# Output projection of a hybrid decoder layer: which engine subtracts and scales, and in which order the second half's products run

## The chip, the cores and the metric

One core of one Trainium2 chip. The time is device microseconds of one execution. Engines: TensorE (PE, its weight loads PEld), VectorE (DVE), ScalarE (ACT), GpSimd (POOL), and SyncE (SP), which here issues DMAs only.

## The reference, cut to what matters

One layer over 1088 tokens (1024 of a prompt, 64 decode tokens), model width 1024, all in float32:

```python
h = x + jnp.concatenate([o_r, o_s], axis=-1) @ w_out
hf = rms_norm(h, norm_ffn_gain)
h = h + jnp.square(jax.nn.relu(hf @ w_up)) @ w_down
```

`o_r` is the retention mixer (8 heads, per-head norm, gate), `o_s` sliding-window attention; each is 512 wide, and `w_out` is 1024 x 1024. `w_up` is 1024 x 4096, `w_down` 4096 x 1024. The outputs also hold the retention states and the window caches.

## The kernel before, in words

Products are made exact enough by splitting: an operand becomes a high part (a rounding cast on ScalarE, line 786) and a low part (source minus high part, a subtraction on VectorE, line 787; `halve`). A product is three matmuls: high x high, low x high and high x low (`mm3`, lines 172 to 174).

Feature-major layout: a tile holds 128 features by tokens. Tokens fall into two halves s = 0, 1 of 544, each of two quarters of Q = 272. The stages are: input projection, attention, retention with the output projection of s = 0 worked into its last three blocks (`out_early`), the output projection of s = 1, then 16 up steps (`up`) and five groups of down products. Up and down use a seven-product scheme: the 2 x 2 block matrix (features in two halves by tokens in two quarters) enters as seven combinations of blocks, so the normalised-to-be rows are needed as operands B11, B21, B22 and the differences T1 to T4.

The output projection of a half makes eight tiles m = 0..7 of 128 output features. For each m, and for each quarter h, 24 matmuls accumulate in one PSUM bank: 12 from the attention half of the input (`a`, weights `woa`) and 12 from the retention half (`r`, weights `wor`). The weights come in pairs (m, m+1) over SP into a ring of three raw tiles (`wo_pair`, line 818) and are split into a ring of four (`wsplit`). `psM` gives eight banks in turn.

- `residual(s, m, pss)`, lines 830 to 853: POOL loads x into one of two `y` buffers (832), DVE adds the two banks (834), which also empties them, POOL stores y to `y_d` for the end of the kernel (836), and f = y * g_ffn is written (842). The returned `squares` squares y on ACT (847, 850) and adds it on DVE to `acc[s]` (851).
- `operands(s, m)`, lines 866 to 887: for a pair m, m + 4 (kk = m % 4) the splits into the operands (`put`, seven) and four differences on POOL (876, 881, 883, 885). The splits read f, some of the differences overwrite f in place.
- `norm(s)`, lines 889 to 897: sums of `acc[s]` over the features by column sums on PE (line 152 through `col_sums`, called at 894), then a power on POOL (132).
- `norm_spread`, lines 899 to 909: PE spreads the result over the partitions (905), ACT copies it to `rsf`. It is used only in `up` (1105).

The driver is lines 1044 to 1076. It first makes the `a` halves of m = 0..3 for s = 1 (all eight banks), then the operands of s = 0 for m = 2, 6, 3, 7. The loop over pairs then makes the `r` halves of (0, 1) and (2, 3), and `a` with `r` for (4, 5) and (6, 7), each followed by `residual`, the remaining operands of s = 0 (list `rest`) and `operands(1, m)`. `norm(0)` follows the pair (2, 3), `norm_spread(0)` the pair (4, 5). With the last pair, the first up weights are loaded, two sums of them made on POOL (1060, 1061) and four of them split; further sums are made at line 1032.

The order of instructions on each engine is made when the program is built: a scheduler simulates the program and takes on each engine, among the instructions that it holds ready, the one written first (`schedule_with_timeline_sim`); `issue_after` ties an instruction behind another. On the chip each engine then keeps to that order.

Of the kernel before, what the change touches and what calls it, by code (L numbers as in the profile page):

```python
# [13 lines left out]
AF = mybir.ActivationFunctionType  # L14
ALU = mybir.AluOpType
# [21 lines left out]
def hymba_layer(ctx: ExitStack, tc: tile.TileContext, a: dict, o: dict):  # L37
    nc = tc.nc
# [19 lines left out]
    def cload(name):  # L58
        t_ = const.tile(list(a[name].shape), F32, name="c_" + name)
        nc.sync.dma_start(t_, a[name])  # L60
        return t_
# [42 lines left out]
    g_ffn = cload("g_ffn")  # L104
# [26 lines left out]
    def rsqrt_inplace(ap, n):  # L131
        nc.gpsimd.tensor_tensor(ap, ap, mhalf.broadcast_to([P, n]), ALU.pow)
# [16 lines left out]
    def col_sums(out, src, rhs):  # L149

        for q in range(0, 128, 32):
            nc.tensor.matmul(out[q : q + 32], src[:, q : q + 32], rhs, start=True, stop=True)
# [34 lines left out]
    def bank(name):  # L187
        pool, tag, n = banks[turn[0] % 8]
        turn[0] += 1
        return pool.tile([P, 512], F32, tag=tag, bufs=n, name=name)  # L190
# [316 lines left out]
    for blk in range(4):  # L507
        w = wload(a["w_in"][3 + blk], 8, f"wqk{blk}")
        dst = qr_d if blk < 2 else kr_d
        for j in range(2):  # L510
            m = (blk % 2) * 2 + j
# [273 lines left out]
    def halve(hi, lo, src, lo_eng):  # L785
        nc.scalar.copy(hi, src)  # L786
        lo_eng.tensor_tensor(lo, src, hi.bitcast(F32), ALU.subtract)  # L787
# [6 lines left out]
    def rawload(src, name, tag="raw", pl=None):  # L794
        if tag == "rawb":
            t_ = ope.tile([P, 4, Q], F32, tag="op" + ("6h", "2h", "2l", "5h", "5l", "6l", "1h", "1l")[kept[0] % 8], name=name)
            raw = t_.rearrange("p k n -> p (k n)")[:, :1024]
            kept[0] += 1
        else:
            raw = mw.tile([P, 1024], F32, tag=tag, name=name, bufs=3)  # L800
        nc.scalar.dma_start(raw, src)
        return raw
# [11 lines left out]
    def wo_pair(s, m, half):  # L814

        raw = mw.tile([P, 1024], F32, tag="raw", name=f"wo{half}{s}_{m}_raw", bufs=3)
        c0 = 512 * (half == "a")
        nc.sync.dma_start(
            raw.rearrange("p (m n) -> p m n", m=2), a["w_out"][m : m + 2, :, c0 : c0 + 512].rearrange("m p n -> p m n")
        )  # L820
        for i in range(2):
            yield wsplit(raw[:, i * 512 : i * 512 + 512], "wa", f"wo{half}{s}_{m + i}", nc.vector)

    def out_half(s, half, ps, h, w, first, last):
        for k in range(4):
            lh, ll = (w[:, i, k * 128 : k * 128 + 128] for i in range(2))
            mh, ml = (mix[s, half + x][:, k, h, :] for x in "hl")
            last_out[0] = mm3(ps, lh, ll, mh, ml, first and k == 0, last and k == 3)

    def residual(s, m, pss):  # L830
        y = om.tile([P, 2, Q], F32, tag="y", name=f"y{s}_{m}", bufs=2)
        nc.gpsimd.dma_start(y.rearrange("p h n -> p (h n)"), a["xY"][:, s, m, :])
        for h in range(2):
            nc.vector.tensor_tensor(y[:, h, :], pss[h], y[:, h, :], ALU.add)
        kk, k2 = m % 4, m // 4
        nc.gpsimd.dma_start(y_d[:, 2 * k2 : 2 * k2 + 2, kk, s, :], y)
        if m > 5 and s == 0:
            f = mx0.tile([P, 2, Q], F32, tag=f"f{m}", name=f"f{s}_{m}")
        else:
            f = om.tile([P, 2, Q], F32, tag=f"f{min(m, 4)}", name=f"f{s}_{m}", bufs=1 + m // 4)  # L840
        fs[s, m] = f
        nc.vector.tensor_scalar(f, y, g_ffn[:, m : m + 1], None, ALU.mult)

        def squares():
            if m == 0:
                acc[s] = mw.tile([P, 2, Q], F32, tag="acc", name=f"acc{s}")
                nc.scalar.activation(acc[s], y, AF.Square)
            else:
                sq = om.tile([P, 2, Q], F32, tag="sq", name=f"sq{s}_{m}")
                nc.scalar.activation(sq, y, AF.Square)  # L850
                nc.vector.tensor_tensor(acc[s], acc[s], sq, ALU.add)

        return squares

    def out_parts(s, ms, half, psum, pss):

        for m in ms:
            if m % 2 == 0:
                gen = wo_pair(s, m, half)
            w = next(gen)  # L860
            for h in range(2):
                if half == "a":
                    pss[m, h] = psum()
                out_half(s, half, pss[m, h], h, w, half == "a", half == "r")

    def operands(s, m):

        kk, k2 = m % 4, m // 4
        f = fs[s, m]

        def put(i, src):
            halve(ops[i][s][0][:, kk, :], ops[i][s][1][:, kk, :], src, nc.vector)

        if k2 == 0:
            put(B11, f[:, 0, :])
            nc.gpsimd.tensor_tensor(f[:, 0, :], f[:, 1, :], f[:, 0, :], ALU.subtract)
            put(T1, f[:, 0, :])
        else:
            put(B21, f[:, 0, :])
            b12, t1 = fs[s, kk][:, 1, :], fs[s, kk][:, 0, :]  # L880
            nc.gpsimd.tensor_tensor(t1, f[:, 1, :], t1, ALU.subtract)
            put(T2, t1)
            nc.gpsimd.tensor_tensor(b12, f[:, 1, :], b12, ALU.subtract)
            put(T3, b12)
            nc.gpsimd.tensor_tensor(f[:, 0, :], f[:, 0, :], t1, ALU.subtract)
            put(T4, f[:, 0, :])
            put(B22, f[:, 1, :])

    def norm(s):

        ps = psM.tile([P, 512], F32, tag="b", name=f"psr{s}")
        for h in range(2):
            for i, r in enumerate((0, 128, 144)):
                col_sums(ps[:, 3 * h + i : 3 * h + i + 1], acc[s][:, h, r : r + 128], ones[:, 0:1])
        rf = (rst, nsinks)[s][:, 0:6]
        nc.vector.tensor_scalar(rf, ps[:, :6], 1.0 / 1024.0, EPS, ALU.mult, ALU.add)
        rsqrt_inplace(rf, 6)
# [124 lines left out]
    def left(order, src, name, lo_eng, raw_tag="raw", raw_pool=None, s_tag="S", s_pool=None, tags=("wa", "wb"), raws=None, sums=None):  # L1022

        r1, r2 = raws or (
            rawload(src[:, i * 1024 : i * 1024 + 1024], f"{name}_r{i + 1}", raw_tag, raw_pool) for i in range(2)
        )
        a11, a12, a21, a22 = r1[:, :512], r1[:, 512:], r2[:, :512], r2[:, 512:]
        have = {1: a11, 2: a12, 4: a22, **(sums or {})}

        def comb(i, p_, q_, op):  # L1030
            t_ = have[i] = (s_pool or mid).tile([P, 512], F32, tag=s_tag, name=f"{name}_s{i}", bufs=10 if s_tag == "Sb" else 4)
            nc.gpsimd.tensor_tensor(t_, p_, q_, op)

        for n, i in enumerate(order):
            if i in (5, 6) and 5 not in have:
                comb(5, a21, a22, ALU.add)
                comb(6, have[5], a11, ALU.subtract)
            if i == 7:
                comb(7, a11, a21, ALU.subtract)
            if i == 3:  # L1040
                comb(3, a12, have[6], ALU.subtract)
            yield wsplit(have[i], tags[n % len(tags)], f"{name}_w{i}", lo_eng)

    late = lambda: bank("pso")
    operand_tiles(0)
    pss = {}
    out_parts(1, range(4), "a", late, pss)
    for m in (2, 6, 3, 7):
        operands(0, m)
    mx0x.close()  # L1050
    operand_tiles(1)
    rest = [0, 4, 1, 5]
    for ms in ((0, 1), (2, 3), (4, 5), (6, 7)):
        if ms[0] > 3:
            out_parts(1, ms, "a", late, pss)
        out_parts(1, ms, "r", late, pss)
        if ms == (6, 7):
            r0 = [rawload(a["w_up"][0][:, i * 1024 : i * 1024 + 1024], f"wu0_r{i + 1}") for i in range(2)]
            s56 = mw.tile([P, 1024], F32, tag="raw", name="wu0_s56", bufs=3)
            nc.gpsimd.tensor_tensor(s56[:, :512], r0[1][:, :512], r0[1][:, 512:], ALU.add)  # L1060
            nc.gpsimd.tensor_tensor(s56[:, 512:], s56[:, :512], r0[0][:, :512], ALU.subtract)
            gen0 = left(
                PROD, None, "wu0", nc.vector, tags=("wa", "wa", "wa", "wa", "wb", "wb", "wb"), raws=r0,
                sums={5: s56[:, :512], 6: s56[:, 512:]})
            ready = [next(gen0) for _ in range(4)]
        for m in ms:
            squares = residual(1, m, [pss[m, h] for h in range(2)])
            if rest:
                operands(0, rest.pop(0))
            operands(1, m)  # L1070
            squares()
        if ms == (2, 3):
            norm(0)
        if ms == (4, 5):
            norm_spread(0, last_out[0])
    ox.close()

# [293 lines left out]
```

## Time and profile before

| | |
|---|---|
| median of 3 runs | 1210.6 us (1209.35 to 1212.11) |
| profiled execution | 1210.2 us, span 1208.4 us |
| granted PE clock, mean over the span | 0.996 |
| matmuls of the output projection, s = 0 | 383.7 to 448.3 us |
| the same, s = 1 | 448.3 to 504.9 us |
| first matmul of the up steps | 504.9 us |

Times on the trace are microseconds from the span's start. In a timeline row stand the start, the time taken, the engine, the line, the operation, its output and inputs, the shape and the count; in brackets the idle time of the engine ahead of it and what ended that. A row of instruction groups ends with the busy time in all, the mean nanoseconds of one, and the idle time ahead of them with its releasers. A row of windows gives for each engine the busy time in that window and, in brackets, the number of instructions, then the granted clock, the share of the DMA engines and GB/s.

### The profile page before, as it was taken

What the parts mean: (1) busy time and instruction counts of PE and PEld (TensorE: products, weight loads), DVE (VectorE), ACT (ScalarE), POOL (GpSimd) and SP (SyncE); (2) the same over time, 40 slices, a digit from 0 to 9 for tenths busy, and PEclk for the clock granted to TensorE, in tenths of its full rate; (3) what the DMA queues carried; (4) which work ended last, traced back from release to release, by engine and by line L of the source; (5) the groups of instructions that cost most, each with busy time, mean ns of one, the idle gap of its engine ahead of it and who ended that gap; (6) DMA issues with size and microseconds to landing.
All of it is one profiled execution on the core that took longest, in us unless ns stands there. A gap on an engine that the chain in (4) does not pass through costs nothing.

```text
span 1208.4 us, 23493 instructions
## 1 busy us (share of the span) xinstructions
PE 1176.6 (97%) x9405; PEld 1128.5 (93%) x9405; DVE 847.7 (70%) x1522; ACT 504.5 (42%) x1039; POOL 522.8 (43%) x433
## 2 busy tenths in 40 slices
PE   8999999999998998899999999999899999999998
PEld 7999998988788998889999999999889998999998
DVE  7557868632366978887666667676578679797776
ACT  8343445543233444454444444444543332424231
POOL 0125333333444535667666766666563132153000
PEclk9999999999999999999999999999999999999999
DMA  6221235244128552434443434444665355543215
GB/s 242 71 61 67 91 101 181 84 146 120 47 79 289 173 163 91 127 125 155 145 154 124 146 132 146 154 145 157 247 229 162 132 171 164 194 150 123 75 57 186
DMA packets 102276, 169.44 MB, mean 140 GB/s; under 512 B 11999, under 2 KB 68255, under 8 KB 101911
## 3 DMA queue, kind: packets, MB, share of 16 engines
q1 hardware_dynamic: 88279, 123.24, 30.6%
q10 hardware_dynamic: 11328, 35.79, 9.2%
q0 software_dynamic: 2560, 8.91, 2.4%
q8 instruction: 74, 1.21, 0.4%
q14 instruction: 35, 0.29, 0.1%
HBM read 114.30 MB, written 53.61 MB: 139 GB/s over the span
## 4 chain that ended last, share of the span: by engine, by line
PE 77%; DVE 10%; DMA 6%; issue 3%; POOL 2%; ACT 1%; SPq 0%; ACTq 0%; DVEq 0%; POOLq 0%
PE psd L173 8%; PE psd L174 7%; PE psd L172 7%; PE psx L172 5%; PE psx L174 5%; PE psx L173 5%; PE psz L172 2%; PE psz L174 2%; PE psz L173 2%; PE pst L172 2%; PE pst L173 2%; PE pst L174 2%; PE psf L172 2%; PE psf L174 2%; PE psf L173 2%
## 5 line engine op out<-in xcount | busy, mean ns | idle before, releaser
L172 PE MATMUL psd<-uh,wd_w 128*128 128x272 f32 x896 | 258.8, 289 | 5.1 <-ACT a L1236 2.4
L173 PE MATMUL psd<-uh,wd_w 128*128 128x272 f32 x896 | 260.1, 290 | 0.9 <-DVE wd_w L787 0.9
L174 PE MATMUL psd<-ul,wd_w 128*128 128x272 f32 x896 | 257.9, 289 | 2.0 <-DVE ul L787 2.0
L172 PEld LDWEIGHTS psd<-uh,wd_w 128*128 128x128 f32 x896 | 169.8, 189 | 5.8 <-ACT a L1236 2.6
L174 PEld LDWEIGHTS psd<-ul,wd_w 128*128 128x128 f32 x896 | 168.8, 189 | 3.3 <-DVE ul L787 3.3
L173 PEld LDWEIGHTS psd<-uh,wd_w 128*128 128x128 f32 x896 | 169.2, 189 | 1.3 <-DVE wd_w L787 1.3
L1240 DVE TENSOR_TENSOR a<-a,psd 128x272 f32<-128x272 f32 x248 | 101.0, 429 | 40.9 <-PE psd L174 40.9
L787 DVE TENSOR_TENSOR wu_w<-wu_s,wu_w 128x512 fp32r<-128x512 f32 x64 | 63.5, 993 | 50.1 <-ACT wu_w L786 49.0
L786 ACT CAST wd_w<-wd_s 128x512 fp32r<-128x512 f32 x64 | 37.3, 618 | 120.5 <-PE psd L174 103.5
L787 DVE TENSOR_TENSOR ul<-ur,uh 128x1088 fp32r<-128x1088 f32 x56 | 81.3, 1479 | 8.0 <-ACT uh L786 8.0
L173 PE MATMUL psx<-op_0h,wu_w 128*128 128x272 f32 x256 | 73.9, 289 | 1.7 <-DVE wu_w L787 1.7
L172 PE MATMUL psx<-op_1h,wu_w 128*128 128x272 f32 x256 | 74.2, 290 | 0.5 <-ACT m L1119 0.5
L172 PE MATMUL psx<-op_0h,wu_w 128*128 128x272 f32 x256 | 74.4, 291 | 0.3 <-ACT m L1119 0.2
L174 PE MATMUL psx<-op_1l,wu_w 128*128 128x272 f32 x256 | 74.1, 289 | 0.0
L174 PE MATMUL psx<-op_0l,wu_w 128*128 128x272 f32 x256 | 74.1, 289 | 0.0
L173 PE MATMUL psx<-op_1h,wu_w 128*128 128x272 f32 x256 | 73.7, 288 | 0.0
L1105 DVE SCALAR_TENSOR_TENSOR m<-m,rsf 128x272 f32<-128x272 f32 x96 | 71.3, 742 | 2.7
L363 POOL TENSOR_TENSOR sp<-sp,ssp 128x1024 f32<-128x1024 f32 (+1 forms) x16 | 28.6, 1788 | 88.4 <-DVE ssp L362 60.1
L786 ACT CAST uh<-ur 128x1088 fp32r<-128x1088 f32 x56 | 59.5, 1099 | 14.7 <-PE psd L173 9.1
L1147 POOL TENSOR_TENSOR r4t<-r3t,r4t 128x272 f32<-128x272 f32 x64 | 64.1, 1012 | 1.2
L172 PE MATMUL psf<-hnh,wqk_hi 128*128 128x384 f32 (+1 forms) x192 | 63.5, 331 | 0.2 <-DVE qkst L515 0.2
L174 PE MATMUL psf<-hnl,wqk_hi 128*128 128x384 f32 (+1 forms) x192 | 63.1, 329 | 0.0
(339 smaller groups left out, 3654.0 us busy)
## 6 DMA issues: line engine op xcount, KB each, us to landing
ur<-u_d SPq DMA_DIRECT2D x52, 544.0 KB, 4.9
u_d<-r4t SPq DMA_DIRECT2D x32, 544.0 KB, 3.7
wu_r<-in_w_up ACTq DMA_DIRECT2D x32, 512.0 KB, 4.3
wd_r<-in_w_down ACTq DMA_DIRECT2D x30, 512.0 KB, 7.3
u_d<-r3t SPq DMA_DIRECT2D x32, 408.0 KB, 3.1
y<-in_xY POOLq DMA_DIRECT2D x16, 272.0 KB, 3.3
y_d<-y POOLq DMA_DIRECT2D x16, 272.0 KB, 3.0
yt<-y_d SPq DMA_DIRECT2D x16, 272.0 KB, 4.1
```

Of the source, the lines that this page charges most:

```text
L172: nc.tensor.matmul(ps, lh, rh, start=first, stop=False, skip_group_check=more)
L173: nc.tensor.matmul(ps, ll, rh, start=False, stop=False, skip_group_check=more)
L174: return nc.tensor.matmul(ps, lh, rl, start=False, stop=last, skip_group_check=more)
L363: nc.gpsimd.tensor_tensor(s, s, ss.unsqueeze(2).broadcast_to([P, 4, n]), ALU.mult)
L786: nc.scalar.copy(hi, src)
L787: lo_eng.tensor_tensor(lo, src, hi.bitcast(F32), ALU.subtract)
L1105: nc.vector.scalar_tensor_tensor(t_, src, 0.0, rsf[:, s, h, :], ALU.max, ALU.mult)
L1147: sub = lambda o_, p_, q_: nc.gpsimd.tensor_tensor(o_, p_, q_, ALU.subtract)
L1240: nc.vector.tensor_tensor(to, to, ps, ALU.add)
```

## The change

Three edits, in `residual`, `operands` and the driver. The scale by g_ffn goes from VectorE to ScalarE (all 16). The four differences go from GpSimd to VectorE (32 in all). In the driver, only the `a` halves of (0, 1) run ahead; `norm(0)` stands right behind them; all later pairs make `a` and then `r`; and `norm_spread(0)` follows the pair (2, 3).

```diff
-        nc.vector.tensor_scalar(f, y, g_ffn[:, m : m + 1], None, ALU.mult)
+        nc.scalar.activation(f, y, AF.Copy, scale=g_ffn[:, m : m + 1])
...
-            nc.gpsimd.tensor_tensor(f[:, 0, :], f[:, 1, :], f[:, 0, :], ALU.subtract)
+            nc.vector.tensor_tensor(f[:, 0, :], f[:, 1, :], f[:, 0, :], ALU.subtract)
...
-            nc.gpsimd.tensor_tensor(t1, f[:, 1, :], t1, ALU.subtract)
+            nc.vector.tensor_tensor(t1, f[:, 1, :], t1, ALU.subtract)
             put(T2, t1)
-            nc.gpsimd.tensor_tensor(b12, f[:, 1, :], b12, ALU.subtract)
+            nc.vector.tensor_tensor(b12, f[:, 1, :], b12, ALU.subtract)
             put(T3, b12)
-            nc.gpsimd.tensor_tensor(f[:, 0, :], f[:, 0, :], t1, ALU.subtract)
+            nc.vector.tensor_tensor(f[:, 0, :], f[:, 0, :], t1, ALU.subtract)
...
-    out_parts(1, range(4), "a", late, pss)
+    out_parts(1, (0, 1), "a", late, pss)
+    norm(0)
...
-        if ms[0] > 3:
+        if ms[0]:
             out_parts(1, ms, "a", late, pss)
         out_parts(1, ms, "r", late, pss)
...
         if ms == (2, 3):
-            norm(0)
-        if ms == (4, 5):
             norm_spread(0, last_out[0])
```

## The prediction

> **What bounds the kernel now.** I read the totals of the page first, then the idle gaps of PE along the span, then the stage around the output projection by windows, then the chain of waits inside it.
>
> ```profile
> span 1208.4 us, 23493 instructions
> PE 1176.6 (97%) x9405; PEld 1128.5 (93%) x9405; DVE 847.7 (70%) x1522; ACT 504.5 (42%) x1039; POOL 522.8 (43%) x433
> ```
>
> TensorE is busy 97% of the span, so an edit to the other engines can win only what PE loses in the stage that it touches. Here is that stage: the second half of the output projection (448.3 to 504.9) and the first up step (504.9 to 536), with one stage of plain up work behind it.
>
> ```profile
> core 0: us, PE busy (x) PEld busy (x) DVE busy (x) ACT busy (x) POOL busy (x), PEclk, DMA share, GB/s
> 448.30:460.20 11.90, 11.90 (x97) 11.90 (x97) 11.73 (x18) 8.60 (x23) 8.16 (x10) 1.00 0.35 107
> 460.20:474.10 13.90, 12.76 (x98) 12.20 (x97) 13.90 (x23) 5.44 (x13) 9.48 (x10) 1.00 0.23 77
> 474.10:488.00 13.90, 10.65 (x117) 10.36 (x116) 9.84 (x20) 6.32 (x14) 7.37 (x9) 0.88 0.55 177
> 488.00:504.90 16.90, 16.90 (x138) 16.90 (x137) 13.85 (x24) 9.10 (x21) 10.74 (x14) 1.00 0.43 131
> 504.90:522.00 17.10, 12.85 (x140) 11.98 (x139) 16.70 (x29) 7.93 (x19) 12.65 (x13) 1.00 0.16 50
> 522.00:536.00 14.00, 12.80 (x95) 11.82 (x95) 11.10 (x17) 7.69 (x18) 6.99 (x5) 1.00 0.43 145
> 536.00:560.00 24.00, 24.00 (x192) 23.90 (x191) 19.23 (x29) 10.68 (x27) 19.61 (x16) 1.00 0.42 156
> 484.00:488.00 4.00, 4.00 (x27) 4.00 (x27) 3.63 (x6) 2.16 (x5) 3.57 (x5) 0.79 0.81 268
> 488.00:492.00 4.00, 4.00 (x35) 4.00 (x34) 3.54 (x9) 1.97 (x4) 1.27 (x3) 1.00 0.37 94
> ```
>
> A matmul takes 24.00 / 192 = 0.125 us in the undisturbed stage. PE is full until 460.2, then loses 1.14, 3.25, 0, 4.25 and 1.20 us, while DVE is busy for 66.0 of the 73.7 us up to 522. In 484 to 488 the granted clock is 0.79 and 27 matmuls run where 4.00 / 0.125 = 32 would.
>
> The gaps, and what ended each:
>
> ```profile
> 468.07 0.40 PE L173 MATMUL pso<-mixr1h,wor 128*128 128x272 f32 x1 [1.02 <-DVE wor L787]
> 482.72 0.59 PE L172 MATMUL pso<-mixah,woa 128*128 128x272 f32 x1 [3.25 <-DVE y L834]
> ...
> 506.79 0.40 PE L173 MATMUL psx<-op_0h,wu_w 128*128 128x272 f32 x1 [1.46 <-DVE wu_w L787]
> 513.09 0.39 PE L172 MATMUL psz<-op_0h,wu_w 128*128 128x272 f32 x1 [1.61 <-ACT wu_w L786]
> 514.31 0.39 PE L173 MATMUL psz<-op_0h,wu_w 128*128 128x272 f32 x1 [0.83 <-DVE wu_w L787]
> 516.29 0.58 PE L152 MATMUL psr<-ones,acc 128*32 128x1 f32 x48 [0.34 <-DVE acc L851]
> ```
>
> Three kinds: 1.02 us behind a weight split on DVE; 3.25 us for a PSUM bank that line 834 had not yet emptied; 1.46 + 1.61 + 0.83 + 0.34 = 4.24 us at up's start behind DVE and ACT work. The chain says why line 834 was late:
>
> ```profile
> 475.15 0.72 POOL f L876
> 475.87 3.00 DMA y_d<-y
> ...
> 479.16 2.97 DMA y<-in_xY
> ...
> 483.31 0.70 POOL y_d L836
> 484.01 4.68 DMA y<-in_xY
> 488.78 0.79 DVE y L834 x2
> ```
>
> There are two y buffers. The y of a pair m must be stored before the y of m + 2 can be loaded, and POOL issues both, behind a subtract. One turn of this ring is 0.79 + 0.70 + 3.00 + 0.3 (the gap 478.87 to 479.16) + 2.97 to 4.68 = 7.8 to 9.5 us for two m. Before, four pairs' `a` halves run first, so the `r` halves of m = 0..3 finish two m every 48 x 0.125 = 6.0 us, faster than the ring turns.
>
> **The change part by part.**
>
> *Order of the second half.* Only two pairs' `a` halves run ahead; after that two m take 96 x 0.125 = 12.0 us, longer than the ring's 9.5. By that pace r(0) ends near 459 (448.3 and 72 matmuls, and the norm) and the load of y(2) lands about 8 us later, near 467; it is needed near 470, and every later turn has 12.0 - 9.5 = 2.5 us or more to spare. So the wait of 3.25 us should go, and with it the slow clock: 5 matmuls short in 484 to 488 is 0.6 us, and I estimate as much for the 1.3 us between 482.7 and 484, which ran in the same state: 1.2. **A = -4.4 us.** No matmul is added or dropped; line 905's and line 152's only move. The bank rotation stays at eight: the third pair's last bank is that of y(2), emptied some 7 us ahead. The weight loads on SP come in the order of use, and in the new order r(0) and r(1) take the ring places that a(2) and a(3) had, so their splits run before 450.
>
> *The first norm moves forward,* between a(1) and r(0). PE is in order, so line 152 now holds everything behind it until the last acc add of the first half is done.
>
> ```profile
> 449.94 6.58 DVE L787 TENSOR_TENSOR op_0l<-f,op_0h 128x272 fp32r<-128x272 f32 x9
> 456.44 1.30 DVE L851 TENSOR_TENSOR acc<-acc,sq 128x544 f32<-128x544 f32 x1
> ...
> 504.44 1.13 DVE L787 TENSOR_TENSOR op_1l<-f,op_1h 128x272 fp32r<-128x272 f32 x3
> ...
> 510.03 0.71 DVE L851 TENSOR_TENSOR acc<-acc,sq 128x544 f32<-128x544 f32 x1
> ```
>
> Before, that add stands behind nine splits and ends at 457.7, with nobody waiting. Now PE gets there at 448.3 + 48 x 0.125 = 454.3. With four subtracts among the nine splits, at the undisturbed 1.13 / 3 = 0.38 us each, DVE reaches the add at 449.9 + 13 x 0.38 = 454.9 and ends it at 455.6: a wait of 1.3 us. The ends are 0 (the add goes earlier) and, with all 14 splits and 8 subtracts of the two kk in front, 449.9 + 22 x 0.38 + 0.71 - 454.3 = 4.7. I take **E = +1.3**, since before nine stood in front and not fourteen. The norm's own row to POOL and its spread follow off PE's path, with two m of matmuls as cover; without that cover they would cost the 0.34 us of the gap at 516.29.
>
> *Subtracts from POOL to DVE, scale from DVE to ACT.*
>
> ```profile
> L787 DVE TENSOR_TENSOR op_0l<-f,op_0h 128x272 fp32r<-128x272 f32 x28 | 18.4, 713 | 0.0
> L787 DVE TENSOR_TENSOR op_1l<-f,op_1h 128x272 fp32r<-128x272 f32 x28 | 15.1, 571 | 1.5 <-ACT op_1h L786 1.5
> L851 DVE TENSOR_TENSOR acc<-acc,sq 128x544 f32<-128x544 f32 x8 | 10.1, 1266 | 0.4 <-ACT sq L850 0.4
> L842 DVE TENSOR_SCALAR f<-y,c_g_ffn 128x544 f32<-128x544 f32 x9 | 5.0, 553 | 0.1
> ...
> L881 POOL TENSOR_TENSOR f<-f,f 128x272 f32<-128x272 f32 x8 | 8.9, 1116 | 2.6 <-DVE op_0l L787 2.2 <-DVE f L842 0.4
> L876 POOL TENSOR_TENSOR f<-f 128x272 f32<-128x272 f32 x8 | 7.6, 954 | 4.7 <-DVE op_1l L787 3.4 <-DVE op_0l L787 1.3
> L885 POOL TENSOR_TENSOR f<-f,f 128x272 f32<-128x272 f32 x8 | 7.4, 940 | 2.2 <-DVE op_1l L787 2.2
> L883 POOL TENSOR_TENSOR f<-f,f 128x272 f32<-128x272 f32 x8 | 7.4, 927 | 0.1
> ...
> L850 ACT ACTIVATE sq<-y 128x544 f32<-128x544 f32 x8 | 5.3, 657 | 5.4 <-DVE y L834 3.6 <-issue 1.7 <-DVE acc L851 0.2
> ...
> L136 ACT ACTIVATE hnh<-x,c_g_mix x24: 557/606/616, 4.4 to 25.8; 128x384 fp32r<-128x384 f32 x16, 128x320 fp32r<-128x320 f32 x8
> ```
>
> POOL loses 8.9 + 7.6 + 7.4 + 7.4 = 31.3 us. DVE gains 32 subtracts at 0.38 = 12.2 us and loses 5.0 us of scaling. Against that, DVE's two-input instructions are far above their undisturbed time while POOL subtracts: 18.4 - 28 x 0.38 = 7.8 for the first row, 15.1 - 10.6 = 4.5 for the second, 10.1 - 8 x 0.71 = 4.4 for the third, 16.7 us in all. That POOL is the cause shows in one line with two forms, later in the kernel, while POOL is busy there too:
>
> ```profile
> L1105 DVE SCALAR_TENSOR_TENSOR m<-m,rsf 128x272 f32<-128x272 f32 x96 | 71.3, 742 | 2.7
> ...
> L1105 DVE SCALAR_TENSOR_TENSOR v<-psx,rsf 128x272 f32<-128x272 f32 x32 | 13.7, 434 | 11.7 <-PE psx L174 11.7
> ```
>
> Reading both inputs from SBUF it takes 742 ns, with one from PSUM 434. The sums for up's first weights (lines 1032, 1060, 1061) stay on POOL and go on disturbing, so I take 14 of the 16.7 as relief: DVE needs 66.0 - 5.0 + 12.2 - 14 = 59 us where it was busy 66. The bounds of the relief are 0 and above 16.7 (the weight splits, not counted, are slowed too).
>
> On ACT the scale costs between the 0.657 of line 850 (same size, no per-partition scale) and 0.616 + 0.15 = 0.77 (line 136's 384 columns with such a scale, plus 160 columns by its slope of about 0.9 ns); I take 0.70. Eight of them are 5.6 us in a stage where ACT is busy 37.4 of 73.7, hidden. In the first half PE runs without a gap, so the eight there earn and cost nothing. Behind a waiting scale on ACT stand the casts for operands and weights; but the cast that wants f comes next anyway, now on the same engine.
>
> With DVE shorter and POOL's queue free of subtracts, the waits of kind one and three shrink. **B**: 1.02 to 0.4, **-0.6** (nothing to all of it: 0 to -1.0). **C**: the 1.61 and 0.83 go, since that weight's cast stood on ACT behind an operand cast waiting for line 881; of the others, as much as 1.6 stays, because up's sums are still POOL's: 4.2 to 1.6, **-2.6** (0 to -4.2). The 1.20 us after 522 wait mostly for weights and copies of the up step and stay.
>
> Sum: -4.4 - 0.6 - 2.6 + 1.3 = **-6.3 us**. The profiled execution took 1210.2 us (span 1208.4 and 1.8 around it), so 1203.9; the median of the runs is 1210.6, 0.4 above it, so **1204.3**. PE is full for most of the rest, so the gain is kept to the end.
>
> **The rivals.**
>
> *The lock pays in full (about 1201).* If POOL's subtracts cost DVE all their time and not just the excess that I could count, B and C vanish whole and the add is never late: -4.4 - 1.0 - 4.2 = -9.6, so 1201.0. The 742 against 434 speaks for it; the sums left on POOL speak against it. The Trainium skill (SBUF — State Buffer, Who interferes with whom) says that a VectorE instruction with two SBUF inputs and a GpSimd instruction that reads SBUF hold a shared port exclusively, the loser blocking for the whole instruction. By that rule this rival gains weight; that the one-input form stands at 434 agrees with it.
>
> *The norm's wait replaces the bank's (about 1209).* All 22 instructions stand ahead of the add: PE waits 4.7 us, long enough for the slow clock's 1.2. Then -4.4 - 0.6 - 2.6 + 5.9 = -1.7, 1208.9. For it: the operands are written ahead of r(0), and DVE was back to back there. Against: nine, not fourteen, stood in front before.
>
> *DVE becomes the bound (slower, 1214.2).* Place: DVE's queue from 449 to up's start. If its slow instructions aren't POOL's doing, DVE needs 66.0 + 12.2 - 5.0 = 73.2 us, 7.2 more, and up's start waits for it as now. It was idle for 73.7 - 66.0 = 7.7 us, partly for the y loads that now come early; whether none or all of that is filled, its end comes 7.2 or 0 us later, and half of it, 3.6, makes 1210.6 + 3.6 = 1214.2. It decides as soon as the relief is below about 3.6 us. The two forms of line 1105, and three splits in 1.13 us at 504.44, speak against it.
>
> *The order doesn't come out as written (about 1207).* The build-time scheduler may still place a(2) and a(3) early; then the 4.4 us of A stay lost, E's wait doesn't arise, and only B and C are won: -3.2, so 1207.4.
>
> **How the numbers follow.** A measurement here can tell about 0.2%, 2.4 us, from no change: 1208.2 to 1213.0. Forecast 0.58, lock in full 0.14, order unchanged 0.08: faster, 0.80. The norm's wait, 0.12: no difference. DVE bound, 0.08: slower. The range from 1200.5 to 1209.5 takes in all but the slower case and the tails; the forecast's own is 1201.5 to 1207, from B, C and E between their ends.
>
> **What would show it.** Right: no PE gap over 1.5 us between 448 and up's first matmul, that matmul some 4 to 5 us earlier than 504.9, clock 1.00 throughout; splits of op_0l and op_1l near 0.43 us, line 876 to 885 on DVE near 0.43; scale on ACT 0.66 to 0.77. Wrong: a long PE gap before line 152 near 454 ended by line 851 (E), DVE full to past 520 (the slower rival), or line 834 still waiting for a y load (A).

## The result, and the profile after

The changed kernel takes 1199.47 us (median of 4 runs, 1198.95 to 1201.61) where the kernel before takes 1211.15 on the same chip (4 runs, 1209.35 to 1212.11): a ratio of 0.990, 95% interval 0.9884 to 0.992. The direction was forecast; the gain of 11.7 us is nearly twice the 6.3 of the sum, and the time lies 1.0 us below the lower end of the range. The profiled execution took 1199.1 us.

Page of the kernel after, totals:

```profile
span 1197.3 us, 23492 instructions
PE 1175.5 (98%) x9405; PEld 1129.0 (94%) x9405; DVE 832.2 (70%) x1538; ACT 512.5 (43%) x1055; POOL 495.4 (41%) x401
```

TensorE's busy time is 1.1 us less than before, the span 11.1. So over the whole span 10 us of PE's idle time went; 6.1 us of them lie between the first output matmul and the first down matmul (9.9 us idle there before, 3.85 after), the others in stages whose code is the same. The windows of the kernel after, second half of the output projection:

```profile
448.40:500.00 51.60, 51.60 (x457) 51.44 (x456) 46.22 (x111) 34.63 (x80) 18.45 (x18) 1.00 0.46 144
```

PE is full there at clock 1.00, and DVE, with the differences now on it, has 51.60 - 46.22 = 5.4 us to spare. These are all of PE's idle gaps between 448 and 560 after the change, in the timeline:

```profile
504.55 0.39 PE L173 MATMUL psz<-op_0h,wu_w 128*128 128x272 f32 x1 [0.67 <-DVE wu_w L787]
...
535.58 0.39 PE L172 MATMUL psx<-op_0h,wu_w 128*128 128x272 f32 x1 [0.17 <-ACT m L1118]
543.40 0.39 PE L172 MATMUL psx<-op_0h,wu_w 128*128 128x272 f32 x1 [3.01 <-ACT m L1118]
```

Set beside the gaps of before: 1.02 and 3.25 in the output projection have become nothing; 4.24 at up's start has become 0.67; and a gap of 3.01 us at 543.4, in the second up step, is new. By stage, from the first matmul of each in the two traces:

| us | before | after | |
|---|---|---|---|
| start of the span to the first output matmul | 383.73 | 384.83 | +1.10 |
| from there to the first up matmul | 121.32 | 114.23 | -7.09 |
| from there to the first down matmul | 342.59 | 339.54 | -3.05 |
| from there to the end | 360.79 | 358.75 | -2.04 |

The first row lies ahead of every changed instruction, and the last row's code is the same in both; in the twelve kernels below, which share that code, it lies anywhere between 355.7 and 359.2. So 10.1 us belong to the change by its place, and 1 us net of the 11.1 does not. Of the 10.1, 1.7 us are a period of half clock at 482 us, which the profile of before has in this stage and that of after has not.

The groups of DVE and ACT after, in the window 448 to 523 that the prediction's rows come from:

```profile
L787 DVE TENSOR_TENSOR op_1l<-f,op_1h 128x272 fp32r<-128x272 f32 x28 | 11.7, 460 | 0.4 <-ACT op_1h L786 0.4
L787 DVE TENSOR_TENSOR op_0l<-f,op_0h 128x272 fp32r<-128x272 f32 x28 | 11.3, 444 | 0.0
...
L851 DVE TENSOR_TENSOR acc<-acc,sq 128x544 f32<-128x544 f32 x8 | 5.8, 720 | 0.0
...
L881 DVE TENSOR_TENSOR f<-f,f 128x272 f32<-128x272 f32 x8 | 3.5, 442 | 0.0
```

```profile
L842 ACT ACTIVATE f<-y,c_g_ffn 128x544 f32<-128x544 f32 x9 | 6.7, 748 | 3.0 <-DVE y L834 3.0
```

The splits fell from 713 and 571 ns to 444 and 460, the adds to `acc` from 1266 to 720, and a difference takes 0.44 us on DVE where it took 0.93 to 1.12 on GpSimd. The scale takes 0.75 us on ACT.

### The profile page after: what moved, and what is told of

It is laid out like the page before. It is cut to its first block, busy times and chain, and to the rows that moved or that the text cites. A ratio compares the mean times of both kernels' runs of the same rounds, so it can differ in the third digit from the quotient of the medians.

```text
span 1197.3 us, 23492 instructions
## 1 busy us (share of the span) xinstructions
PE 1175.5 (98%) x9405; PEld 1129.0 (94%) x9405; DVE 832.2 (70%) x1538; ACT 512.5 (43%) x1055; POOL 495.4 (41%) x401
## 4 chain that ended last, share of the span: by engine, by line
PE 79%; DVE 7%; DMA 4%; issue 3%; POOL 3%; ACT 2%; SPq 0%; ACTq 0%; DVEq 0%; POOLq 0%
PE psd L173 8%; PE psd L174 8%; PE psd L172 8%; PE psx L172 4%; PE psx L174 4%; PE psx L173 4%; PE pst L172 2%; PE psz L172 2%; PE psz L174 2%; PE psz L173 2%; PE pst L173 2%; PE pst L174 2%; PE psf L172 2%; PE psf L174 2%; PE pso L173 2%
```

## The experiments

The theory after seeing this: GpSimd's differences were slowing VectorE's two-input instructions, and VectorE's lateness was behind the waits of all three kinds, the bank's among them. The rival is that of the prediction: the order of the products removes the bank wait, and the differences only shorten up's start. A third question is where the 3.01 us at 543.4 come from, and a fourth why the norm did not make PE wait.

The ratio is to the kernel before on the same chip. The idle columns are sums of PE's idle gaps of 0.1 us or more in each profile: those before up's first matmul, those of up that end on the copy of a product on ACT (line 1118 after, 1119 before), and the others of up to 560. A slow period is 3.41 us at a granted clock of 0.50; the last column counts those between 448 and 560, and one of 6.83 us (in e2, e3, e6 and e7) as two.

| kernel | median us | ratio [95%] | idle, projection | idle, up, others | idle, up, copy | slow periods |
|---|---|---|---|---|---|---|
| before | 1209.6 to 1211.7 | | 4.40 | 4.59 | 0.78 | 1 |
| changed | 1199.47 | 0.9902 [0.9884, 0.992] | 0 | 0.67 | 3.18 | 0 |
| e1, order alone | 1208.18 | 0.9972 [0.9958, 0.9985] | 2.35 | 4.90 | 0.60 | 2 |
| e2, differences alone | 1204.50 | 0.9948 [0.9931, 0.9965] | 0 | 2.49 | 2.40 | 3 |
| e3, scale alone | 1209.60 | 0.9988 [0.9972, 1.0004] | 6.02 | 2.52 | 1.11 | 2 |
| e4, order and differences | 1200.01 | 0.9908 [0.9890, 0.9926] | 0 | 1.33 | 1.54 | 0 |
| e5, changed, norm late | 1203.46 | 0.9948 [0.9930, 0.9966] | 0 | 2.22 | 2.51 | 2 |
| e6, before, no residual load | 1205.56 | 0.9964 [0.9952, 0.9977] | 2.07 | 3.71 | 0 | 2 |
| e7, changed, with idle subtracts on GpSimd | 1207.69 | 0.9980 [0.9966, 0.9993] | 0 | 5.52 | 2.04 | 4 |
| e8, changed, first up step's differences on DVE | 1198.53 | 0.9898 [0.9880, 0.9917] | 0 | 0.58 | 1.90 | 1 |
| e9, changed, two weight sums on DVE | 1197.38 | 0.9895 [0.9876, 0.9915] | 0 | 0 | 2.20 | 1 |
| e10, norm late and the sums on DVE | 1200.83 | 0.9920 [0.9904, 0.9937] | 0 | 1.20 | 2.19 | 0 |
| e11, e8 and e9 together | 1194.40 | 0.9868 [0.9847, 0.9889] | 0 | 0 | 0.94 | 0 |
| e12, changed, again | 1199.05 | 0.9911 [0.9892, 0.9929] | 0 | 0.87 | 3.23 | 1 |

### e1: the order alone

```diff
-    out_parts(1, range(4), "a", late, pss)
+    out_parts(1, (0, 1), "a", late, pss)
+    norm(0)
...
-        if ms[0] > 3:
+        if ms[0]:
...
-            norm(0)
-        if ms == (4, 5):
             norm_spread(0, last_out[0])
```

> Only the order of the second half (two m ahead, pairs whole, first norm behind them); subtracts stay on GpSimd, the scale on VectorE. Theory 1, the losses add up and each edit removes its own: the 3.25 us bank wait and its slow clock go, the waits behind VectorE and ScalarE at up's start stay: about 4 to 6 us faster than before. Theory 2, one cause: VectorE slowed by GpSimd's subtracts is late everywhere, so with the bank wait gone the same time is lost behind VectorE's splits or the acc add before the norm: within 2 us of before.

Measured 0.9972, some 3.4 us, between the two theories. Its idle gaps of over 0.5 us, from PE's timeline:

```profile
456.71 0.58 PE L152 MATMUL psr<-ones,acc 128*32 128x1 f32 x48 [1.77 <-DVE acc L851]
...
480.50 0.37 PE L172 MATMUL pso<-mixah,woa 128*128 128x272 f32 x1 [0.58 <-DVE y L834]
...
504.91 0.39 PE L173 MATMUL psx<-op_0h,wu_w 128*128 128x272 f32 x1 [2.95 <-DVE wu_w L787]
512.51 0.39 PE L173 MATMUL psz<-op_0h,wu_w 128*128 128x272 f32 x1 [1.29 <-DVE wu_w L787]
```

The bank wait fell from 3.25 to 0.58. That is what the ring's turn asked for, but e1 does not show it by itself: the new order also puts fewer VectorE instructions ahead of the first add of line 834 (22 where before has 32), so that add comes at 463.47 and not at 471.45, and the ring starts 7.2 us earlier, counted from the first output matmul of each. In exchange the norm of the first half, moved forward, waits 1.77 us for the last add to `acc`: that is the wait that the prediction put at 1.3 and that the whole change does not show. Up's start waits as long as before, and VectorE's splits are as slow (means of 719 and 734 ns in the window 448 to 523).

### e2: the differences alone

```diff
-            nc.gpsimd.tensor_tensor(t1, f[:, 1, :], t1, ALU.subtract)
+            nc.vector.tensor_tensor(t1, f[:, 1, :], t1, ALU.subtract)
...
```

(and the same for the other three; the order of before, the scale on VectorE).

> Only the 32 subtracts on VectorE; old order, scale on VectorE. Theory 1: the waits at up's start and behind the weight split go, the bank wait stays since the y ring is as before: 4 to 7 us faster, with a gap of some 2 to 3 us behind line 834 still there. Theory 2: nearly the whole gain of the change, 9 to 12 us, also the bank wait, because GpSimd's queue no longer holds up the loads and stores of y. Rival of the forecast, VectorE the bound: slower than before.

Measured 0.9948, some 6.3 us: nearly twice what the order gives. It is the gain of the first theory with the bank wait gone as in the second. PE's gaps of over 0.3 us:

```profile
502.30 0.39 PE L172 MATMUL psz<-op_0h,wu_w 128*128 128x272 f32 x1 [0.48 <-ACT wu_w L786]
504.70 0.39 PE L173 MATMUL psz<-op_0h,wu_w 128*128 128x272 f32 x1 [2.01 <-DVE wu_w L787]
...
545.81 0.39 PE L172 MATMUL psx<-op_0h,wu_w 128*128 128x272 f32 x1 [2.22 <-ACT m L1119]
```

The bank wait is gone in the old order, with the `a` halves of m = 0..3 ahead (the "four pairs" of the prediction). Two stretches of DVE's timeline say how. First the kernel before:

```profile
460.24 2.29 DVE L787 TENSOR_TENSOR op_0l<-f,op_0h 128x272 fp32r<-128x272 f32 x3
462.45 1.25 DVE L787 TENSOR_TENSOR wor<-wor_raw,wor 128x512 fp32r<-128x512 f32 x1
463.63 3.22 DVE L787 TENSOR_TENSOR op_0l<-f,op_0h 128x272 fp32r<-128x272 f32 x4
...
471.45 0.43 DVE L834 TENSOR_TENSOR y<-pso,y 128x272 f32<-128x272 f32 x1
```

and then e2:

```profile
461.24 0.43 DVE L881 TENSOR_TENSOR f<-f,f 128x272 f32<-128x272 f32 x1
461.59 0.68 DVE L787 TENSOR_TENSOR wor<-wor_raw,wor 128x512 fp32r<-128x512 f32 x1
...
463.60 0.43 DVE L834 TENSOR_TENSOR y<-pso,y 128x272 f32<-128x272 f32 x1
```

In before a split takes 2.29 / 3 = 0.76 to 3.22 / 4 = 0.80 us and a weight split 1.25; in e2 a difference takes 0.43 and a weight split 0.68, and the mean of the splits to op_0l is 432 ns. The first add of line 834, which starts the ring of two y buffers, comes at 471.45 in the one and 463.60 in the other, 7.9 us sooner (6.7 counted from the first output matmul of each), where PE had waited 3.25. This is the time of the instructions and not their number: from the last such add of the first half to this one, VectorE has 32 instructions in 23.0 us before and 41 in 16.5 us in e2, back to back in both. So the ring was not only slower than the products, it had started late.

### e3 and e4: the scale

e3 is the kernel before with the scale moved, e4 is the changed kernel with the scale put back on VectorE:

```diff
-        nc.vector.tensor_scalar(f, y, g_ffn[:, m : m + 1], None, ALU.mult)
+        nc.scalar.activation(f, y, AF.Copy, scale=g_ffn[:, m : m + 1])
```

> Only the scale on ScalarE. Both theories: VectorE loses 5 of 66 busy us in the stage, little of it where PE waits; within 1.5 us of before. If over 2 us faster, VectorE's queue length by itself was the bound at up's start.

> The whole change but for the scale, which stays on VectorE. Both theories: within 1.5 us of the changed kernel (10 to 12 us faster than before). If the scale matters, 2 us or more behind the changed kernel, with VectorE late at up's start.

e3's interval takes in 1, and e4 (0.9908) stands where the whole change stands (0.9902). The scale is worth nothing that these runs can tell, in either place. In e3 PE's bank wait is even longer in the profile (4.52 us behind line 834, against 3.25): DVE's splits are as slow as before, so taking 0.55 us off its queue at each m frees nobody.

The two parts that matter: e1 gives 3.4 us, e2 6.3, together 9.7; e4 gives 11.1. With intervals of 1.6 to 2.2 us either way on each, the sum of the two and the pair together cannot be told apart in the total. In single waits they do not add: the bank wait is 3.25 before, 0.58 with the one, 0 with the other, 0 with both.

### e6: a shorter ring

The kernel before, without the load of x into y and with a copy in place of the add of line 834, so that its output lacks the residual x; everything else is as before.

```diff
-        nc.gpsimd.dma_start(y.rearrange("p h n -> p (h n)"), a["xY"][:, s, m, :])
...
-            nc.vector.tensor_tensor(y[:, h, :], pss[h], y[:, h, :], ALU.add)
+            nc.vector.tensor_copy(y[:, h, :], pss[h])
```

> The kernel before without the loads of x into y: line 834 becomes a copy out of PSUM, so the output lacks the residual x, and a buffer of y needs no load after its store. Theory 1 (the ring of two y buffers makes the bank wait): the 3.25 us gap ended by line 834 goes or falls below 1 us though VectorE is as late as before, and 3 to 5 us are won. Theory 2 (VectorE's lateness alone makes it): a bank wait of 2 us or more stays.

Measured 0.9964. The summary of its line 833 between 452 and 500 us (the copy; minimum, median and maximum in ns, first and last start) is:

```profile
L833 DVE COPY y<-pso x12: 424/429/441, 472.2 to 495.0; 128x272 f32<-128x272 f32 x12
```

The first read of the banks comes at 472.2, as late as before, and still no gap of PE is ended by that line. What is left in the projection are waits for weight splits, 0.48 and 1.59 us, and up's start waits as before. So the bank wait needed both things, a ring that turns slowly and a start that is late; the ring or the differences alone remove it, and the order alone all but 0.58 us of it.

### e7: GpSimd reads again, for nothing

The changed kernel with 24 extra subtracts on GpSimd, one beside each difference that belongs to a pair m > 3. Their result goes to a place that is written again before it is used; in the traces TensorE, VectorE and ScalarE run the same instructions in the same order as in the changed kernel.

```diff
             nc.vector.tensor_tensor(t1, f[:, 1, :], t1, ALU.subtract)
+            if m > 3: nc.gpsimd.tensor_tensor(rsf[:, 1, 0, :], f[:, 1, :], f[:, 1, :], ALU.subtract)
...
```

> The changed kernel, and beside each VectorE difference for m = 4..7 (24 of the 32) a subtract of the same size on GpSimd that reads f twice and writes a place that is overwritten later; nobody needs its result. If GpSimd's reading alone slows VectorE's two-input instructions: op_0l, op_1l and acc in the stage rise from about 0.43 and 0.72 us to a mean of 0.55 or more and 1.0, and 3 to 7 us of the gain are lost. If the dependence on GpSimd's results made the loss and not the sharing: splits near 0.43, and less than 1.5 us lost.

Measured 0.9980: of 11.9 us (0.98% of the kernel before's 1210.6) 2.4 are left. DVE's groups, in the same window as above:

```profile
L787 DVE TENSOR_TENSOR op_1l<-f,op_1h 128x272 fp32r<-128x272 f32 x28 | 14.1, 544 | 0.4 <-ACT op_1h L786 0.4
L787 DVE TENSOR_TENSOR op_0l<-f,op_0h 128x272 fp32r<-128x272 f32 x28 | 12.5, 481 | 0.0
...
L851 DVE TENSOR_TENSOR acc<-acc,sq 128x544 f32<-128x544 f32 x8 | 6.7, 837 | 0.0
...
L885 DVE TENSOR_TENSOR f<-f,f 128x272 f32<-128x272 f32 x8 | 5.9, 735 | 0.0
L882 DVE TENSOR_TENSOR f<-f,f 128x272 f32<-128x272 f32 x8 | 5.6, 706 | 0.4 <-ACT f L842 0.3
```

and the gaps of PE that came back:

```profile
503.27 0.59 PE L173 MATMUL psx<-op_0h,wu_w 128*128 128x272 f32 x1 [2.14 <-DVE wu_w L787]
...
512.32 0.39 PE L173 MATMUL psz<-op_0h,wu_w 128*128 128x272 f32 x1 [2.77 <-DVE wu_w L787]
515.00 0.82 PE L152 MATMUL psr<-ones,acc 128*32 128x1 f32 x48 [0.61 <-DVE acc L851]
```

and VectorE's timeline ahead of the first of them:

```profile
491.70 0.44 DVE L834 TENSOR_TENSOR y<-pso,y 128x272 f32<-128x272 f32 x1 [2.14 <-DMA y<-in_xY]
...
499.69 2.92 DVE L787 TENSOR_TENSOR op_1l<-f,op_1h 128x272 fp32r<-128x272 f32 x3
```

Nobody waits for the extra subtracts' results. VectorE's splits, adds and differences are slower again: 14.1 - 11.7, 12.5 - 11.3, 6.7 - 5.8 and, for the two lines of differences, 5.6 + 5.9 - 2 x 3.5 make 9.0 us. Up's start waits 5.5 us for VectorE, where it was 4.6 in the kernel before. (Four slow periods behind these gaps, against none in the changed kernel's profile, are part of the price.) The sizes written down were off: the means rose to 481, 544 and 837 ns, less than 0.55 and 1.0 us, and more than 3 to 7 us of the gain went. This is the experiment that carries the theory: GpSimd's reading, with the order of the other engines unchanged, costs most of the gain. One rival is not quite shut out. The extra subtracts may also hold back what stands behind them in GpSimd's queue, the y stores and loads. PE has no gap at line 834, but VectorE waited 2.14 us for one load of y, at 491.70, where its longest such wait in the changed kernel is 0.68 (1.20 in e12); from there to the split that PE waited for it worked without a pause, three splits taking 2.92 us where three take 1.14 in the changed kernel. How much of the loss belongs to that one wait is not separated. The Trainium skill (SBUF — State Buffer, Who interferes with whom) has the rule by which this goes: a VectorE instruction with two SBUF inputs contends with a GpSimd instruction that reads SBUF, for a port pair that is locked and not shared out. These runs agree with it, by the 9.0 us above.

### e5 and e10: where the norm stands

e5 is the changed kernel with the norm behind the pair (2, 3) and the spread behind (4, 5), as before; e10 is the same with the two weight sums of e9.

```diff
-    norm(0)
...
         if ms == (2, 3):
+            norm(0)
+        if ms == (4, 5):
             norm_spread(0, last_out[0])
```

> The changed kernel, but the first norm and its spread stay where they were (behind the pairs (2, 3) and (4, 5)). The forecast's term E (a wait of PE before the early norm, 1.3 us) would make this faster than the changed kernel by about 1 us. Both theories now: the changed kernel shows no gap there, so the same as the changed kernel within 1.5 us (11 to 12 us faster than before).

> As e9, but the first norm and its spread where they were before the change. Theory 1: the late norm of e5 cost time only because there GpSimd's sums came first at 492.6 and held up VectorE by some 2.5 us, not by the norm itself: then within 1.5 us of e9, and the gap of 2.05 us behind the weight split at up's start gone. Theory 2: the place of the norm matters by itself (its power and copies collide with up's start): 3 us or more slower than e9.

With the differences on VectorE the early norm costs nothing: neither in the changed kernel nor in e5 does the norm of the first half make PE wait. Against what was expected, the late norm is slower, by 0.0046 in the ratio against the changed kernel (e5), by 0.0025 against e9 (e10, where the intervals overlap). For e5 the profile places it: gaps of 0.43 and 1.79 us at 504 to 506, with a slow period behind them, and another behind that of 2.51. For e10 it does not: from the first output matmul to the first down matmul it needs 453.1 us, e9 453.0; what its profile is longer by lies in stages with the same code, though the medians too are 3.5 us apart. So what the place of the norm does to e10 stays open.

### e8, e9, e11, e12: what is left at up's start

e8 puts the differences of the first up step on VectorE, e9 the two weight sums of lines 1061 and 1062, e11 both; e12 is the changed kernel once more.

```diff
-                sub = lambda o_, p_, q_: nc.gpsimd.tensor_tensor(o_, p_, q_, ALU.subtract)
+                sub = lambda o_, p_, q_: (nc.gpsimd if fp else nc.vector).tensor_tensor(o_, p_, q_, ALU.subtract)
...
-            nc.gpsimd.tensor_tensor(s56[:, :512], r0[1][:, :512], r0[1][:, 512:], ALU.add)
-            nc.gpsimd.tensor_tensor(s56[:, 512:], s56[:, :512], r0[0][:, :512], ALU.subtract)
+            nc.vector.tensor_tensor(s56[:, :512], r0[1][:, :512], r0[1][:, 512:], ALU.add)
+            nc.vector.tensor_tensor(s56[:, 512:], s56[:, :512], r0[0][:, :512], ALU.subtract)
```

> The changed kernel with the eight differences of the first up step (line 1146) on VectorE too. If the new gap of 3.01 us before the second up step's third product comes from GpSimd, whose queue holds those differences behind sums that wait for a weight load, while the buffer of the squares is single: the gap goes, 2 to 4 us faster than the changed kernel. Otherwise the gap stays and VectorE's 8 x 0.43 = 3.4 us come out as nothing or as up to 2 us slower.

> The changed kernel with the two sums for up's first weights (lines 1061 and 1062 there) on VectorE too, so that no two-input work of GpSimd meets VectorE between 450 and up's start. If the sharing is what is left there: the 5.7 us that line 1061 took on GpSimd falls to 0.7 on VectorE, the gap of 0.67 us ended by a weight split goes, 0 to 3 us faster than the changed kernel. If VectorE is too full for two more of 0.69 us: gaps behind it at up's start, 1 us or more slower.

> e9 and e8 together: all of GpSimd's arithmetic that meets this stage on VectorE. If both waits are GpSimd's, 2 to 4 us faster than the changed kernel (1195 to 1198). If VectorE is the bound by then, the same as the changed kernel or slower.

> The changed kernel itself, on the same chip as e9 to e11: 10 to 13 us faster than before. Its profile shows what repeats: if the gap before the second up step's third product and the clock's half speed are the same as in the first profile, they belong to the kernel; if they differ, to the execution.

Two views of the changed kernel lead to these. GpSimd's timeline, where one sum takes 5.71 us and the next of the same shape 1.30:

```profile
491.12 5.71 POOL L1061 TENSOR_TENSOR wu_s<-wu_r 128x512 f32<-128x512 f32 x1 [0.73 <-DVE wor L787]
496.79 0.56 POOL L832 DMA_DIRECT2D y<-in_xY  x1
497.36 1.30 POOL L1062 TENSOR_TENSOR wu_s<-wu_s,wu_r 128x512 f32<-128x512 f32 x1
...
529.42 1.29 POOL L1032 TENSOR_TENSOR wu_s<-wu_r 128x512 f32<-128x512 f32 x1 [5.97 <-DMA wu_r<-in_w_up]
```

and ACT's:

```profile
498.70 0.62 ACT L786 CAST wu_w<-wu_s 128x512 fp32r<-128x512 f32 x1 [3.51 <-POOL wu_s L1062]
...
541.08 0.43 ACT L1105 ACTIVATE r3t<-m 128x272 f32<-128x272 f32 x1 [4.75 <-POOL r4t L1146]
...
542.98 0.66 ACT L1118 COPY m<-psx 128x272 f32<-128x272 f32 x2
```

The sum at 491.12 ran beside VectorE's two-input instructions, which stood back to back, and took 4.4 us longer than its like; the cast of that weight waited 3.51 us for the sums, and PE's 0.67 at 504.55 is what came of it. With the sums on VectorE (e9) that gap is gone. The gap at 543.40 waits for the copy of line 1118, which stands in ACT's queue behind the squares of line 1105; there is one buffer for a square, and GpSimd's differences of the first up step (1146) still read it, since they stand behind sums that waited 5.97 us for a weight's load. With those differences on VectorE (e8) the gap falls from 3.01 to 1.90, with the sums alone (e9) to 2.20; with both (e11) this is PE's one gap:

```profile
536.50 0.39 PE L172 MATMUL psx<-op_1h,wu_w 128*128 128x272 f32 x1 [0.94 <-ACT m L1118]
```

So in e8 the gap was cut and did not go, as it was to. By themselves e8 (0.9898) and e9 (0.9895) cannot be told from the changed kernel. Together, at 0.9868, they can: on the same chip e12, the changed kernel, has 0.9911, and the two intervals do not overlap (1194.40 us against 1199.05). A second buffer for the squares, which would test that wait without touching GpSimd, and more y buffers, for the ring, were not tried.

e12 repeats the changed kernel's time (1199.05) and its gaps, 0.87, 0.22 and 3.01 where the first profile has 0.67, 0.17 and 3.01, so these belong to the kernel and not to one execution.

## Why the prediction was right and wrong, point by point

**A, the order, -4.4: the wait went, the cause was too narrow.** The gap of 3.25 us and the slow period behind it are gone. What was wrong is that the order alone got the credit: for the kernel before, the prediction asked how fast the ring turns and not when it starts. Its start was late by VectorE's slow splits, and the differences alone (e2) take the wait away too; e6 shows that a shorter ring does as much. The pace of the products, on which A rests, no run shows by itself, since in e1 (3.25 to 0.58) the ring also starts earlier. Nor was there the spare time foretold: in the changed kernel the load of y(2) was issued at 469.74, behind work of ScalarE, where it was to have landed near 467 (468 with this profile's later start), and VectorE added it at 472.97; no gap of PE came of that. The slow period was 3.41 us at 0.50, 1.7 us and not the 1.2 that was estimated from the missing matmuls.

**E, the norm's wait, +1.3: did not come, by the scheduler's doing.** DVE's timeline after:

```profile
454.94 0.72 DVE L851 TENSOR_TENSOR acc<-acc,sq 128x544 f32<-128x544 f32 x1
```

The add starts at 454.94 and ends at 455.66; the prediction said 454.9 and 455.6 (the stage starts 1.1 us later in this profile, so counted from there the add came that much sooner). Not the add was mis-sized but PE's arrival, "PE gets there at 454.3": the scheduler put line 152 behind the first 24 matmuls of r(0), so PE reached it at 457.95, after the add, as PE's timeline has it:

```profile
457.60 0.29 PE L173 MATMUL pso<-mixr1h,wor 128*128 128x272 f32 x1
457.73 0.29 PE L174 MATMUL pso<-mixr1l,wor 128*128 128x272 f32 x1
457.95 0.58 PE L152 MATMUL psr<-ones,acc 128*32 128x1 f32 x48
```

Without those 24 matmuls PE would have come at 457.95 - 24 x 0.125 = 454.95 and waited some 0.7 us, by this estimate. In e1, where 12 matmuls stand in front and the splits are slow, the wait is there, 1.77 us. So that E came to nothing is in part the scheduler's placing, which the prediction had not looked for, and in part the differences, which bring the add forward.

**B, -0.6: 1.02 became 0,** its outer bound, with the weight splits of `wor` at 692 ns in the changed kernel's window, where they took 877 before.

**C, -2.6: mis-sized, and by more than its own term.** The relief of VectorE was sized well: 18.4 - 11.3 for the one row of splits, 15.1 - 11.7 for the other and 10.1 - 5.8 for the adds are 14.8 us against the 14 taken. What was mis-sized is the next step, "as much as 1.6 stays, because up's sums are still POOL's": of 4.24 us 0.67 stayed. The 1.20 us after 522, which were to stay, fell to 0.17 by 536. Against that, 3.01 us came up at 543.4, a wait that no part of the prediction names. In the kernel before ScalarE waited for the same differences only 0.75 us, twice, at 550 to 551, and PE not at all; I take it that PE's own lateness covered the wait, which no run shows by itself. Together these leave C at -1.5 by brackets (5.37 to 3.85 us).

**The scale** took 0.75 us, inside 0.657 to 0.77 and above the 0.70 taken, and cost nothing, as argued.

**The sum.** By the brackets, idle time of PE between 448 and 560 fell from 9.77 to 3.85 us, 5.9; with the slow period 7.6. The stage rows say 10.1. The rest is that a bracket tells less than the gap costs: matmuls start 0.125 us apart and are shown as 0.29 long (457.60 and 457.73 above), so that at 468.07 the bracket says 1.02 and the starts lie 1.18 beyond their usual distance, and the matmul behind a gap starts some 0.23 us after it. Counted by starts, every distance above 0.22 us, what lies beyond 0.125 fell from 13.3 to 4.9 us, 8.4; with the slow period that is 10.1, all that the stage rows say.

So the step that failed is the one under the whole sum, which took the bracket as the price of a wait. With each edit's true effect in brackets the sum would have been 7.6 and not 6.3, and that difference is about E, the 1.3 that did not come (A and B won 1.1 more than stated, C 1.1 less, which is luck). From 7.6 to 10.1 is the price that brackets leave out. The last 1.6 us, from there to the 11.7 of the medians, lie in stages with the same code and between the profiles and the medians; nothing here gives them a cause.

**The rivals.** The lock paying in full (1201.0) was nearest, and its mechanism is the one that e7 speaks for; it too took its prices from brackets. VectorE as the bound did not arise: its relief was 14.8 us where 3.6 would have decided. The norm's wait in place of the bank's was real in e1 alone.

## What to carry to other kernels

The differences on GpSimd were paid twice here, in GpSimd's time and in that of VectorE's two-input instructions beside them. In another kernel, compare the mean of one form of VectorE's instructions where GpSimd is busy and where it is not, and count the excess as the price of GpSimd's work. When a wait ends on a ring of buffers, look at when the ring starts as well as at how fast it turns; the two have different cures, and either may do. When waits ahead of a stage go, look in the stage behind it for work that was ready only because PE was late.

## What the runs showed of the hardware

The slowing works both ways. A GpSimd sum of 128x512 that takes 1.30 us took 5.71 (5.72 in e12) while VectorE issued two-input instructions back to back. This is VectorE at the end of that sum in the changed kernel:

```profile
495.61 0.43 DVE L834 TENSOR_TENSOR y<-pso,y 128x272 f32<-128x272 f32 x1
495.96 1.18 DVE L787 TENSOR_TENSOR op_1l<-f,op_1h 128x272 fp32r<-128x272 f32 x1
```

The add at 495.61 is VectorE's first instruction since the sum began that has one input in PSUM. The sum ends 1.22 us after that add starts, and the split behind the add takes 1.18 us where its like takes 0.43; e12 has the same at 493.38. I read this as the sum getting in there. In e5, where the scheduler's order let the sums in first, they took 1.30 and 1.38, and two splits of VectorE beside the first took 2.15 us together where two take 0.79. The Trainium skill (SBUF — State Buffer, Who interferes with whom) says that it is the order of issue that decides who blocks. e5 agrees; in the changed kernel the sum is shown from 491.12, ahead of ten VectorE instructions that start after it and are not slowed. That many short instructions of VectorE hold one of GpSimd off for 4.4 us is this trace's.

The same gap of PE was followed by a slow period in one execution and not in another. Windows behind the 3.01 us gap, first in the changed kernel's profile and then in e12's:

```profile
544.70:548.20 3.50, 3.50 (x30) 3.50 (x29) 3.44 (x4) 0.79 (x4) 3.42 (x3) 1.00 0.35 144
```

```profile
542.50:546.00 3.50, 3.50 (x18) 3.50 (x18) 3.10 (x4) 0.81 (x4) 3.42 (x3) 0.51 0.37 152
```

In 3.50 us 30 matmuls run in the one and 18 in the other. Gaps as short as 1.77 us (e1, at 456.71) and 1.90 (e8) had such a period behind them, and one of 2.19 (e10) had none. Each slow period costs 3.41 x 0.5 = 1.7 us; both profiled executions of the main comparison have three in all, at about 380, 482 and 885 before and 310, 382 and 860 after. So in these runs a gap of some 1.8 us or more has a price of its length and, in part of the executions, 1.7 us more, or 3.4 where the period is 6.83 us long; one profile cannot tell which part.
